# Grouped score matmuls in the mixer, the second token tile on ScalarE's queue, and a later mean product in the two feed-forward stages

## The chip, the core and the metric

The kernel runs on one core of one Trainium2 chip. The metric is the device time of one execution in microseconds (us), the median of several runs. The kernel before took 804.68 us (three runs, 804.41 to 805.51).

## What is computed

One layer of a streaming encoder on 512 tokens of 1024 channels, all in float32:

```
x = x + 0.5 * (silu(h @ w_gate) * (h @ w_up)) @ w_down      # FFN1, h = rms(x) * gain, 1024 -> 2816 -> 1024
x = x + concat(attention(q, k, v), pool(u)) @ w_out         # mixer, [q k v u] = rms(x) * gain @ w_in
x = x + 0.5 * (silu(h @ w_gate) * (h @ w_up)) @ w_down      # FFN2, with its own gain and weights
out = rms(x) * gain
```

The norm is `rms(x) = x * rsqrt(mean(x*x) + 1e-6)` over the channels of a token. The attention has 8 heads of 64 channels. Its queries and keys are normalized head by head, and each chunk of 64 tokens attends to itself and the chunks before it, with a learned bias and a softmax. The pooling branch takes trailing means over 2, 4, 8 and 16 tokens, and a small linear map of them.

## The kernel before

**Products in three parts.** TensorE (PE) multiplies fp32r operands. To reach float32 accuracy each operand is split: ScalarE (ACT) casts it to a high part (line 132, or line 471 in the later half of the feed-forward stages), and VectorE (DVE) subtracts that from the original and gets a low part (line 133 or 476). A product (`mm3`) is then three matmuls, on lines 198 (high, high), 199 and 200 (one low part in each). Channels lie on partitions and tokens in the free dimension, in 8 tiles `x[k]` of 128 channels by 512 tokens; the code calls one such tile a token tile.

**Feed-forward stage (`ffn_up`, used for FFN1 and FFN2).** It begins with four PSUM banks, `first[0..3]`, into which the products of all 8 tiles `k` are added. The weights come in four pieces of 128x1024 (`weights`, for `kp` 0 to 3, two values of `k` each); a piece is asked for on SyncE's queue (line 181), cast by ACT and subtracted by DVE. The very first piece of FFN1 comes in four quarters, so that the first product need not wait for all of it. In FFN1 the tiles of x are asked for between the weight pieces, also on SyncE's queue (line 842). In FFN2 x is already there.

**The norm is applied late.** The products use `x * gain`; the factor of each token, `rb`, is multiplied in afterwards. `acc` collects the squares of x (line 305). `Norm.finish` makes `rb` from it:

```
finish: matmul(wide, mean_of, acc)                   # line 334, PE, the "mean product"
rough:  Ln, Exp, Square                              # lines 318 to 320, ACT
exact:  two scalar_tensor_tensor operations -> rb    # lines 324 and 328, DVE
```

`rb` has two kinds of users, all on DVE: `evacuate`, which empties the `first` banks and those of later plain products (lines 418 and 422; until it has run, the banks are not free for further products), and `norm.blocks`, which scales the eight tiles of x by `rb` (line 359), adds and subtracts blocks of them (line 365) and splits the results into `xa`, `sa` and `ha`, the operands of the rest of the stage. That rest uses, for each group f of 256 columns, seven products on sums of blocks in place of eight; the sums of weight blocks, `wsum`, are made by DVE too (lines 494, 500 and 501). In FFN2 the squares are collected as the mixer's end produces x, so `acc` is nearly ready when the stage begins.

**What sets the order.** Every engine executes its instructions strictly in its program order. In the feed-forward stages a list scheduler of the tile framework puts each engine's instructions in order; what is emitted under `tc.high_priority()` is put ahead of other ready work. In the kernel before, `norm.finish()` is called under it, mean product and all, ahead of the products of `k` = 6. The split tiles, `parts`, have three places; a cast into one waits until PE has used the last weights that lay there.

**Mixer.** Here a planner of the kernel's own (`plan`) lists jobs with costs and ranks, simulates the five engines with the kernel's buffers, among them the 8 PSUM banks (`room`), and writes the order that comes out. `RANK` gives the priorities (the lower first), `SLOW` a factor on the planned costs of ACT and DVE. A score job multiplies the queries of a pair of heads with their keys (line 1528, 64-row operands, results of 64 to 512 columns). It takes 2 banks and consists of 6 matmuls; a pair has 4 of them, 24 matmuls, and there are 4 pairs. The results are evacuated (`evac`), biased, put through a softmax by ACT, transposed by PE (line 1592) and multiplied with v (line 1618). Between the runs of score matmuls PE does products of `mm3` for other heads and for the pooling branch. The planner counts 0.2 us for each change between the two kinds.

Of the kernel before, what the change touches and what calls it, by code (L numbers as in the profile page):

```python
# [8 lines left out]
F32 = mybir.dt.float32  # L9
F32R = mybir.dt.float32r  # L10
I32 = mybir.dt.int32
AF = mybir.ActivationFunctionType
ALU = mybir.AluOpType
# [6 lines left out]
KD = D // P  # L20
# [23 lines left out]
ORDER = (0, "v", 1, "u", "u", "u", "u")  # L44
RANK = dict(
    weights=(-1.0, 0.905, 3.0), qk=2.0, turn=1.1, head=0.9, pool=0.965, map=0.95, u=2.0,
    score=0.5, evac=0.3, bias=1.2, wp=1.1, add=1.1, next=0.965,
)
HOP = 0.45
SLOW = dict(act=1.1, dve=1.06)  # L50
T_MM3 = 0.655
MIX_ENGINES = {
    mybir.EngineType.PE, mybir.EngineType.DVE, mybir.EngineType.Activation, mybir.EngineType.Pool,
# [3 lines left out]
def layer(  # L57
# [31 lines left out]
    nc = tc.nc  # L89
# [39 lines left out]
    def split(src, hi, lo, scale=None):  # L129

        if scale is None:
            nc.scalar.copy(hi, src)  # L132
            nc.vector.tensor_tensor(lo, src, hi.bitcast(F32), op=ALU.subtract)  # L133
        else:
            nc.scalar.activation(hi, src, AF.Copy, scale=scale)
            nc.vector.scalar_tensor_tensor(
                lo, src, scale, hi.bitcast(F32), op0=ALU.mult, op1=ALU.subtract
            )
# [36 lines left out]
    def weights(src, parts=1):  # L175
        n = src.shape[-1]
        raw = raw_tile()
        hi, lo = part_tiles()
        for i in range(parts):
            part = slice(i * n // parts, (i + 1) * n // parts)  # L180
            nc.sync.dma_start(raw[:, part], src[:, part])
            split(raw[:, part], hi[:, part], lo[:, part])
        return hi, lo

    def ordered(acc):
# [16 lines left out]
    def cut(pair, lo, n):  # L202
        return pair[0][:, lo : lo + n], pair[1][:, lo : lo + n]
# [9 lines left out]
    x = residual_tiles()  # L213
    x_d = dram.tile([2 * NT, P, S], F32, name="x_d")

    gain_sb = const.tile([P, 3, KD], F32, name="gain_sb")
    nc.scalar.dma_start(gain_sb, gains)
    ident = const.tile([P, P], F32, name="ident")
    make_identity(nc, ident)
    mean_of = const.tile([P, P], F32R, name="mean_of")  # L220
# [7 lines left out]
    def tables(func, after):  # L228

        if func == AF.Ln:  # L230
            with tc.manual_schedule(engines={mybir.EngineType.Activation}):
                nc.scalar.copy(table, after)
                nc.scalar.preload_act_table_set("natural_log_exp_and_others")
        else:
            nc.scalar.activation(table, after, func, scale=0.0)
# [48 lines left out]
    class Norm:  # L284
# [47 lines left out]
        def finish(self):  # L332
            wide, y, y2 = abank(), temp(), temp()
            nc.tensor.matmul(
                wide.rearrange("p (i a) -> p i a", a=2), mean_of.bitcast(F32),
                self.acc.rearrange("p (a i) -> p i a", a=2), start=True, stop=True,
            )
            self.rough(wide, y, y2)
            tables(AF.Silu, y[:, 0:1])
            self.exact(wide, y, y2)  # L340

        def blocks(self, pool, aside):

# [62 lines left out]
    def ffn_up(norm, wA, down, loaded, in_order, plain, turns=()):  # L406
# [21 lines left out]
        for kp in range(KD // 2):  # L428
            if not loaded:
                load(2 * kp)  # L430
            w = weights(wA[kp], 1 if loaded or kp else 4)
            if not loaded:
                load(2 * kp + 1)
                norm.square(2 * kp)
                norm.square(2 * kp + 1)
            if kp == KD // 2 - 1:
                with tc.high_priority():
                    norm.finish()
            for kk in range(2):
                k = 2 * kp + kk  # L440
                for j in range(4):
                    mm3(first[j], cut(w, (kk * 4 + j) * P, P), norm.h[k], k == 0, k == KD - 1)
        for k in turns:
            z = temp()
            turn_blocks(z, k)
            put_aside(z, k)
# [126 lines left out]
        with tc.manual_schedule(engines={E.PE, E.DVE, E.Activation}):  # L573
            last_silu = last_place = last_sums = nothing
            for n in range(plain, KF):
                f = down.order[n]
                acc, up_lo, up_hi = bank()[:, :HT], bank()[:, :HT], abank()[:, :HT]
                u, z, sg = temp(), temp(), temp()
# [260 lines left out]
    n1, n2, n3 = Norm(0), Norm(1), Norm(2)  # L839

    def load(k):
        nc.sync.dma_start(x[k], xT[k])
        n1.add(k, square=False)


# [15 lines left out]
    with tc.tile_pool(name="act1", bufs=1, reuse_waits="tile") as apool, ExitStack() as in_order:  # L861
# [52 lines left out]
        for g in range(G):  # L914
            now = ahead
# [24 lines left out]
    with tc.tile_pool(name="mix", bufs=1, reuse_waits="tile") as mpool:  # L940
# [12 lines left out]
        class Job:  # L953
            def __init__(self, engine, cost, rank, emit, after, gets, uses, lag, chunk):
                self.engine, self.cost, self.rank, self.emit = engine, cost, rank, emit
                self.after = [z for z in after if z is not None]
                self.gets, self.uses, self.lag, self.chunk = gets, uses, lag, chunk
                self.no, self.then, self.waits, self.ready = len(jobs), [], 0, 0.0

        def job(engine, cost, rank, emit, after=(), gets=(), uses=(), lag=0.0, chunk=None):  # L960
            z = Job(engine, cost, rank, emit, after, gets, uses, lag, chunk)
# [39 lines left out]
        def plan():  # L1001
            free = dict(pe=2.0, act=0.0, dve=0.0, pool=0.0, sp=0.0)
            slots = {what: [-1.0] * n for what, (n, _) in room.items()}
            turn_of = dict(raw=0)
            where, left, open_jobs = {}, dict(held_by), {e: [] for e in free}
            order, times, now = [], [], 0.0
            chunk, scoring, pooling = 0, False, 0.0
            for z in jobs:
                if not z.waits:
                    open_jobs[z.engine].append(z)  # L1010

            def rooms_for(z):
                need, got = {}, []
                for what, key in z.gets:
                    if key in where:
                        continue
                    ready = [t is not None and t <= now for t in slots[what]]
                    n = need.get(what, 0)
                    need[what] = n + 1
                    if what in turn_of:  # L1020
                        i = (turn_of[what] + n) % len(ready)
                        if not ready[i]:
                            return None
                    else:
                        fit = sorted((slots[what][i], i) for i, ok in enumerate(ready) if ok)
                        if len(fit) <= n:
                            return None
                        i = fit[n][1]
                    got.append((what, key, i))
                return got  # L1030

            while len(order) < len(jobs):
                moved = False
                for e in free:
                    if free[e] > now:
                        continue
                    best = None
                    for z in open_jobs[e]:
                        if z.ready > now:
                            continue  # L1040
                        rank = z.rank(chunk) if callable(z.rank) else z.rank
                        if best is None or (rank, z.no) < best[:2]:
                            got = rooms_for(z)
                            if got is not None:
                                best = rank, z.no, z, got
                    if best is None:
                        continue
                    z, got = best[2:]
                    open_jobs[e].remove(z)
                    for what, key, i in got:  # L1050
                        slots[what][i], where[key] = None, (what, i)
                        if what in turn_of:
                            turn_of[what] = (i + 1) % len(slots[what])
                    cost = z.cost * SLOW.get(e, 1.0)
                    if e == "pe":
                        score = z.rank == RANK["score"]
                        cost, scoring = cost + 0.2 * (score != scoring), score
                        chunk = max(chunk, z.chunk or 0)
                    elif e == "pool":
                        pooling = now + cost  # L1060
                    free[e] = now + cost
                    end = now + cost + z.lag + HOP
                    times += [free[e], end]
                    order.append((z, got))
                    z.t0, z.t1 = now, now + cost
                    moved = True
                    for key in z.uses:
                        left[key] -= 1
                        if not left[key]:
                            what, i = where.pop(key)  # L1070
                            slots[what][i] = end
                    for k in z.then:
                        k.waits, k.ready = k.waits - 1, max(k.ready, end if k.engine != e else free[e])
                        if not k.waits:
                            open_jobs[k.engine].append(k)
                if not moved:
                    times = [t for t in times if t > now]
                    now = min(times)
            return order
# [986 lines left out]
```

## Time and profile before

| | |
|---|---|
| median of the runs | 804.68 us (804.41 to 805.51) |
| the profiled execution, its own time | 804.5 us |
| its span in the trace | 802.7 us |
| TensorE busy | 793.5 us (99%) |
| VectorE busy | 709.3 us (88%) |
| ScalarE busy | 499.7 us (62%) |
| GpSimd busy | 152.5 us (19%) |

The span is what the trace covers; 1.8 us of the execution's own time lie outside it. The stages follow each other on PE: the four first banks of FFN1 from 4.8 us, the mixer from about 319 to 483 us, FFN2 from 483 to 796 us, then the last norm and the output. In a row of the timeline stand the start, the duration, the engine, the line, the operation, out<-in by the names of the program, tile and form, the count of like instructions in the row, and in brackets how long the engine was idle before and what ended that. PE is pipelined: a 128x512 matmul lasts 0.38 us in its row but the next begins 0.216 us later (256 columns: 0.11 us).

### The profile page before, as it was taken

The page shows a single profiled execution, that of the slowest core. Times are in us where ns is not written, and L with a number is a line of the kernel's source. Part 1 is how long each engine was busy: PE and PEld are TensorE (multiplying, and loading weights), DVE is VectorE, ACT ScalarE, POOL GpSimd, SP SyncE. Part 2 cuts the span into 40 slices and gives each one's busy share as a digit, 9 for nine tenths or more (in the row PEclk, how much of TensorE's full clock was granted, in tenths as well). Part 3 has the DMA queues.
Part 4 walks back from the last instruction along what each step waited for, and adds up shares of the span by engine and source line. Part 5 has one row for each costly group of instructions (what it writes and reads, how often), then busy time and mean ns, then how long its engine had stood idle before and what let it go on. Part 6 is the DMA issues. An engine that isn't in the chain of part 4 may idle for free.

```text
span 802.7 us, 14916 instructions
## 1 busy us (share of the span) xinstructions
PE 793.5 (99%) x5706; PEld 745.4 (93%) x5706; DVE 709.3 (88%) x1112; ACT 499.7 (62%) x857; POOL 152.5 (19%) x240
## 2 busy tenths in 40 slices
PE   9999999999999999999999999999999999999996
PEld 7889999999999999888888888899999999988986
DVE  7999999999987997778789688999999999986997
ACT  8456655556675675559769545455666655766584
POOL 0023212223220000231444263101110011200010
PEclk9999999999999999999999999999999999999999
DMA  8266889879999675585764867236666457869642
GB/s 291 77 210 210 239 229 245 216 187 259 241 293 317 220 212 156 183 255 100 189 197 81 185 155 204 105 115 205 168 160 195 159 171 175 259 238 343 210 141 105
DMA packets 73848, 158.57 MB, mean 198 GB/s; under 512 B 6560, under 2 KB 31664, under 8 KB 73392
## 3 DMA queue, kind: packets, MB, share of 16 engines
q1 hardware_dynamic: 49808, 109.09, 40.2%
q0 software_dynamic: 23680, 48.24, 28.5%
q8 instruction: 45, 0.74, 0.4%
q10 hardware_dynamic: 288, 0.27, 0.1%
q14 instruction: 27, 0.22, 0.1%
HBM read 153.38 MB, written 50.34 MB: 254 GB/s over the span
## 4 chain that ended last, share of the span: by engine, by line
PE 89%; DVE 5%; issue 1%; DMA 1%; ACT 1%; SPq 0%; DVEq 0%; ACTq 0%
PE mm L200 18%; PE mm L198 18%; PE mm L199 18%; PE a L198 11%; PE a L199 11%; PE a L200 10%; DVE aside L359 1%; PE mm L1528 1%; DVE parts L133 1%; PE mm L1592 1%; DMA raw<-in_wA_dram 1%; DVE aside L365 1%; PE a L1618 1%; PE mm L1618 1%; PE a L1592 0%
## 5 line engine op out<-in xcount | busy, mean ns | idle before, releaser
L565 ACT ACTIVATE t<-mm 128x256 f32<-128x256 f32 x105 | 40.5, 386 | 112.0 <-PE mm L200 110.0
L132 ACT CAST parts<-raw 128x1024 fp32r<-128x1024 f32 (+2 forms) x77 | 74.1, 968 | 51.4 <-PE mm L199 16.6
L133 DVE TENSOR_TENSOR parts<-raw,parts 128x1024 fp32r<-128x1024 f32 (+2 forms) x77 | 85.7, 1121 | 14.8 <-ACT parts L132 14.1
L714 POOL COPY mark<-t 128x1 f32<-128x1 f32 x40 | 16.4, 410 | 331.4 <-DVE t L609 247.7
L199 PE MATMUL mm<-ha,parts 128*128 128x256 f32 x280 | 77.0, 275 | 0.0
L200 PE MATMUL mm<-ha,parts 128*128 128x256 f32 x280 | 77.0, 275 | 0.0
L198 PE MATMUL mm<-ha,parts 128*128 128x256 f32 x280 | 77.0, 275 | 0.0
L716 POOL DMA_DIRECT2D wsum<-in_wB_dram x72 | 70.7, 1114 | 22.5 <-DMA wsum<-wsum 15.0
L476 DVE TENSOR_TENSOR parts<-wsum,parts 128x1024 fp32r<-128x1024 f32 x53 | 64.5, 1218 | 5.1 <-ACT parts L471 5.1
L471 ACT CAST parts<-wsum 128x1024 fp32r<-128x1024 f32 x53 | 53.8, 1046 | 0.8 <-DVE wsum L494 0.4
L198 PEld LDWEIGHTS mm<-ha,parts 128*128 128x128 f32 x280 | 53.8, 192 | 0.1
L199 PEld LDWEIGHTS mm<-ha,parts 128*128 128x128 f32 x280 | 53.8, 192 | 0.1
L200 PEld LDWEIGHTS mm<-ha,parts 128*128 128x128 f32 x280 | 53.8, 192 | 0.0
L133 DVE TENSOR_TENSOR ah<-acts,ah 128x512 fp32r<-128x512 f32 (+1 forms) x72 | 47.1, 662 | 3.0 <-ACT ah L132 2.9
L200 PE MATMUL mm<-hhi,parts 128*128 128x512 f32 x120 | 45.9, 385 | 0.5 <-DVE parts L133 0.5
L198 PE MATMUL mm<-hhi,parts 128*128 128x512 f32 x120 | 45.4, 382 | 0.7 <-DVE t L418 0.3
L199 PE MATMUL mm<-hlo,parts 128*128 128x512 f32 x120 | 46.0, 385 | 0.0
L132 ACT CAST ah<-acts 128x512 fp32r<-128x512 f32 (+1 forms) x72 | 40.8, 580 | 8.3 <-PE mm L199 6.4
L476 DVE TENSOR_TENSOR parts<-raw,parts 128x512 fp32r<-128x512 f32 (+1 forms) x52 | 43.4, 858 | 0.0
L494 DVE TENSOR_TENSOR wsum<-raw 128x1024 f32<-128x1024 f32 x35 | 42.6, 1218 | 0.0
L1116 ACT CAST parts<-raw 128x1024 fp32r<-128x1024 f32 x24 | 25.1, 1046 | 25.8 <-DMA raw<-in_wQK_dram 6.0
L471 ACT CAST parts<-raw 128x512 fp32r<-128x512 f32 (+1 forms) x52 | 39.2, 754 | 2.9 <-DMA raw<-in_wA_dram 2.9
(332 smaller groups left out, 3066.5 us busy)
## 6 DMA issues: line engine op xcount, KB each, us to landing
raw<-in_wA_dram SPq DMA_DIRECT2D x87, 512.0 KB, 4.5
wsum<-in_wB_dram POOLq DMA_DIRECT2D x60, 512.0 KB, 6.9
raw<-wsum SPq DMA_DIRECT2D x36, 512.0 KB, 5.1
raw<-in_wB_dram SPq DMA_DIRECT2D x30, 512.0 KB, 4.7
wsum<-wsum POOLq DMA_DIRECT2D x20, 512.0 KB, 4.5
x<-in_xT_dram SPq DMA_DIRECT2D x16, 256.0 KB, 6.2
raw<-in_wQK_dram SPq DMA_DIRECT2D x8, 512.0 KB, 4.0
wsum<-in_wB_dram POOLq DMA_DIRECT2D x12, 256.0 KB, 6.9
```

Of the source, the lines that this page charges most:

```text
L132: nc.scalar.copy(hi, src)
L133: nc.vector.tensor_tensor(lo, src, hi.bitcast(F32), op=ALU.subtract)
L198: nc.tensor.matmul(acc, a[0], high, start=start, stop=False, **more)
L199: nc.tensor.matmul(acc, a[0], low, start=False, stop=False, **more)
L200: nc.tensor.matmul(acc, a[1], high, start=False, stop=stop, **more)
L471: nc.scalar.copy(hi, src)
L476: nc.vector.tensor_tensor(lo, src, hi.bitcast(F32), op=ALU.subtract)
L494: nc.vector.tensor_tensor(z, raw[:, : 2 * S], raw[:, S : 3 * S], op=ALU.add)
L565: nc.scalar.activation(natural(dst), ordered(src), AF.Copy, scale=scale)
L714: nc.gpsimd.tensor_copy(mark[:, 0:1], after[:, 0:1])
L716: nc.gpsimd.dma_start(self.rows(i, g), self.rows(self.terms[i][at], g), **(dict(accum_op=ALU.add) if at else {}),)
L1116: return lambda: nc.scalar.copy(buf["part", i][0], buf["raw", i])
```

## The change

Four edits:

1. **Mixer.** The rank of `evac` goes from 0.3 to 0.9, and the planned slowness of ACT from 1.1 to 1.06. A new test, `worth`, holds a score job back unless the job before it on PE was a score job too, or enough PSUM banks are free for `GROUP` = 2 score jobs of its pair (or as many as are left of it).
2. **Start of FFN1.** `x[1]` is asked for on ScalarE's queue, behind the gains, and no longer on SyncE's.
3. **First quarter of the first weight piece.** Its cast goes from ACT to DVE (`tensor_copy`). Everything else in `weights` stays.
4. **Mean product.** `norm.finish()` is called after the first product (three matmuls) of `k` = 6 rather than ahead of all of them, and only what follows the mean product (`rough`, the Silu table, `exact`) stands under `tc.high_priority()`. This holds for FFN1 and FFN2.

```
-    score=0.5, evac=0.3, bias=1.2, wp=1.1, add=1.1, next=0.965,
+    score=0.5, evac=0.9, bias=1.2, wp=1.1, add=1.1, next=0.965,
-SLOW = dict(act=1.1, dve=1.06)
+GROUP = 2
+SLOW = dict(act=1.06, dve=1.06)
...
-            split(raw[:, part], hi[:, part], lo[:, part])
+            if i == 0 and parts > 1:
+                nc.vector.tensor_copy(hi[:, part], raw[:, part])
+                nc.vector.tensor_tensor(
+                    lo[:, part], raw[:, part], hi[:, part].bitcast(F32), op=ALU.subtract
+                )
+            else:
+                split(raw[:, part], hi[:, part], lo[:, part])
...
     nc.scalar.dma_start(gain_sb, gains)
+    nc.scalar.dma_start(x[1], xT[1])
...
-            self.rough(wide, y, y2)
-            tables(AF.Silu, y[:, 0:1])
-            self.exact(wide, y, y2)
+            with tc.high_priority():
+                self.rough(wide, y, y2)
+                tables(AF.Silu, y[:, 0:1])
+                self.exact(wide, y, y2)
...
-            if kp == KD // 2 - 1:
-                with tc.high_priority():
-                    norm.finish()
             for kk in range(2):
                 k = 2 * kp + kk
                 for j in range(4):
                     mm3(first[j], cut(w, (kk * 4 + j) * P, P), norm.h[k], k == 0, k == KD - 1)
+                    if (kp, kk, j) == (KD // 2 - 1, 0, 0):
+                        norm.finish()
...
-        nc.sync.dma_start(x[k], xT[k])
+        if k != 1:
+            nc.sync.dma_start(x[k], xT[k])
...
+            def worth(z):
+                if scoring or z.engine != "pe" or z.rank != RANK["score"]:
+                    return True
+                more = min(GROUP, sum(k.t0 is None for k in of_pair[z.uses[0]]))
+                return sum(t is not None and t <= now for t in slots["bank"]) >= 2 * more
...
-                        if best is None or (rank, z.no) < best[:2]:
+                        if (best is None or (rank, z.no) < best[:2]) and worth(z):
```

In the changed kernel the same code has other line numbers: `mm3` 205 to 207, the mean product 342, `rough` 326 to 328, `exact` 332 and 336, scores 1549, splits 134 and 137.

**PE at the start of FFN2.** In the listings the tile numbers are unique: mm_6109 to mm_6112 are the four first banks, hhi_5900, hhi_5915 and so on to hhi_6025, hhi_6079 and hhi_6094 are the tiles of x in the order of use, acc_5908 is the sum of squares, a_6203 (6206) the mean product's bank. Before, the mean product stands 16 matmuls into the stage:

```order
L200 MATMUL mm_6112<-hhi_5900,parts 128x512
L198 MATMUL mm_6109<-hhi_5915,parts 128x512
L199 MATMUL mm_6109<-hlo_5916,parts 128x512
L200 MATMUL mm_6109<-hhi_5915,parts 128x512
L198 MATMUL mm_6110<-hhi_5915,parts 128x512
L334 MATMUL a_6203<-acc_5908,mean_of 128x512
L199 MATMUL mm_6110<-hlo_5916,parts 128x512
L200 MATMUL mm_6110<-hhi_5915,parts 128x512
```

Now it stands behind the first product of `k` = 6:

```order
L207 MATMUL mm_6112<-hhi_6025,parts 128x512
L205 MATMUL mm_6109<-hhi_6079,whi_6198 128x512
L206 MATMUL mm_6109<-hlo_6080,whi_6198 128x512
L207 MATMUL mm_6109<-hhi_6079,wlo_6199 128x512
L342 MATMUL a_6206<-acc_5908,mean_of 128x512
L205 MATMUL mm_6110<-hhi_6079,whi_6198 128x512
L206 MATMUL mm_6110<-hlo_6080,whi_6198 128x512
```

It was PE's row 3465 and is now its row 3524: 59 matmuls later, not three, since before it was put ahead of products that the program names first.

**DVE at the same place.** raw_6141 and raw_6197 are weight pieces of the first banks, raw_6269, raw_6302 and raw_6363 those of the next plain products, raw_6375 the one whose block sums wsum_6415 and wsum_6439 are. Before:

```order
L133 TENSOR_TENSOR parts<-raw_6141,parts 128x1024
L133 TENSOR_TENSOR wlo_6199<-raw_6197,whi_6198 128x1024
L928 STREAM_TRANSPOSE t_6238<-x_2849 128x512
L928 STREAM_TRANSPOSE t_6244<-x_2849 128x512
L324 SCALAR_TENSOR_TENSOR t_6205<-a_6203,t_6205 128x512
L133 TENSOR_TENSOR parts<-raw_6269,parts 128x1024
L328 SCALAR_TENSOR_TENSOR rb_6212<-t_6205,t_6204 128x512
L359 SCALAR_TENSOR_TENSOR aside_6264<-x_2846,gain_sb,rb_6212 128x512 x2
L359 SCALAR_TENSOR_TENSOR aside_6264<-x_2847,gain_sb,rb_6212 128x512 x2
L133 TENSOR_TENSOR parts<-raw_6302,parts 128x1024
```

Now:

```order
L134 TENSOR_TENSOR parts<-raw_6141,parts 128x1024
L134 TENSOR_TENSOR wlo_6199<-raw_6197,whi_6198 128x1024
L134 TENSOR_TENSOR parts<-raw_6269,parts 128x1024
L134 TENSOR_TENSOR parts<-raw_6302,parts 128x1024
L134 TENSOR_TENSOR parts<-raw_6363,parts 128x1024
L502 TENSOR_TENSOR wsum_6415<-raw_6375 128x1024
L937 STREAM_TRANSPOSE t_6238<-x_2849 128x512
L332 SCALAR_TENSOR_TENSOR t_6208<-a_6206,t_6208 128x512
L937 STREAM_TRANSPOSE t_6244<-x_2849 128x512
L336 SCALAR_TENSOR_TENSOR rb_6215<-t_6208,t_6207 128x512
L508 TENSOR_TENSOR wsum_6439<-wsum_6415,raw_6375 128x512
L427 TENSOR_TENSOR t_6250<-mm_6109,rb_6215 128x512
```

Three weight splits and two sums of weight blocks that stood behind the first operation of `exact` now stand at it or ahead of it; every scaling of x stands behind it as before.

In the mixer, PE's score matmuls stood in 8 runs of 6, 18, 6, 12, 6, 24, 18 and 6; in the changed kernel they stand in 5 runs of 18, 6, 24, 24 and 24.

More of the change, by code (lines that the diff above doesn't have):

```diff
@@ L958, in __init__ @@
                 self.no, self.then, self.waits, self.ready = len(jobs), [], 0, 0.0
+                self.t0 = self.t1 = None
         def job(engine, cost, rank, emit, after=(), gets=(), uses=(), lag=0.0, chunk=None):
@@ L1007, in plan @@
             chunk, scoring, pooling = 0, False, 0.0
+            of_pair = {}
+            for z in jobs:
+                if z.engine == "pe" and z.rank == RANK["score"]:
+                    of_pair.setdefault(z.uses[0], []).append(z)
+            def worth(z):
[3 more added lines that the diff above has]
+                return sum(t is not None and t <= now for t in slots["bank"]) >= 2 * more
             for z in jobs:
```

## The prediction

> **What bounds the kernel now.** I read the busy shares of the page first, then its chain of work that ended last.
>
> ```profile
> span 802.7 us, 14916 instructions
> PE 793.5 (99%) x5706; PEld 745.4 (93%) x5706; DVE 709.3 (88%) x1112; ACT 499.7 (62%) x857; POOL 152.5 (19%) x240
> PE 89%; DVE 5%; issue 1%; DMA 1%; ACT 1%; SPq 0%; DVEq 0%; ACTq 0%
> ```
>
> PE is busy all the time, so only two things move the end: fewer microseconds of PE work, or PE waiting for somebody. Only 9 us are not PE. The candidate for making PE wait is DVE at 88%, and an average hides where it is full. So I took the windows table by stage; the columns are window, length, then busy time of PE, PE's weight loads, DVE, ACT and POOL, then the granted clock, DMA share and GB/s.
>
> ```profile
> 420.00:440.00 20.00, 20.00 (x124) 17.59 (x121) 18.62 (x57) 18.30 (x45) 9.11 (x12) 1.00 0.45 80
> 480.00:500.00 20.00, 19.95 (x90) 16.60 (x89) 16.20 (x21) 10.90 (x14) 9.45 (x15) 1.00 0.69 188
> 500.00:520.00 20.00, 19.67 (x91) 16.93 (x90) 19.96 (x26) 8.83 (x12) 2.64 (x2) 1.00 0.28 95
> 520.00:540.00 20.00, 20.00 (x151) 19.07 (x150) 19.71 (x30) 13.35 (x23) 1.70 (x4) 1.00 0.44 142
> ```
>
> From 500 to 540 us, the start of FFN2, DVE idles 0.33 us in 40: there is no room, and any time that DVE loses just before is not made up there. In the mixer ACT and DVE are both above 90%. These two places and FFN1's start are what the change touches.
>
> **FFN2, the mean product.** The timelines of PE, ACT and DVE there:
>
> ```profile
> 486.76 1.34 PE L334 MATMUL a<-acc,mean_of 128*128 128x512 f32 x2
> 505.70 0.45 PE L198 MATMUL mm<-hhi,parts 128*128 128x512 f32 x1 [0.33 <-DVE t L418]
> 538.95 0.28 PE L200 MATMUL mm<-xa,parts 128*128 128x256 f32 x1
> ...
> 488.20 0.69 ACT L318 ACTIVATE t<-a,eps 128x512 f32<-128x512 f32 x1
> 489.99 0.72 ACT L319 ACTIVATE t<-t,less_ln 128x512 f32<-128x512 f32 x1
> 491.55 0.62 ACT L320 ACTIVATE t<-t 128x512 f32<-128x512 f32 x1
> 494.83 1.05 ACT L132 CAST parts<-raw 128x1024 fp32r<-128x1024 f32 x1 [1.14 <-PE mm L199]
> 500.01 1.05 ACT L132 CAST parts<-raw 128x1024 fp32r<-128x1024 f32 x1 [4.13 <-PE mm L199]
> ...
> 492.48 0.65 DVE L324 SCALAR_TENSOR_TENSOR t<-a,t 128x512 f32<-128x512 f32 x1
> 514.97 1.22 DVE L133 TENSOR_TENSOR wlo<-raw,whi 128x1024 fp32r<-128x1024 f32 x1
> 537.11 1.22 DVE L476 TENSOR_TENSOR parts<-wsum,parts 128x1024 fp32r<-128x1024 f32 x1
> ...
> L494 DVE TENSOR_TENSOR wsum<-raw 128x1024 f32<-128x1024 f32 x35 | 42.6, 1218 | 0.0
> ```
>
> The order moves the mean product back by 59 matmuls. At 0.216 us each that is 12.7 us; PE is otherwise back to back, so it runs at about 499.5 in place of 486.76. Nothing in between depends on it. The Ln began 1.44 us after the mean product started (488.20 - 486.76); then come 0.69 + 0.72 + 0.62 us of ACT, now in one piece, because the casts stand ahead of them. So the first operation of `exact` can start at 499.5 + 1.44 + 2.03, about 503.0, in place of 492.48: 10.5 us later. If casts still fell between, it would be the old distance, 492.48 - 486.76 = 5.72, hence 505.2.
>
> DVE works in order, and what does it do meanwhile? The new order puts three splits and one sum of weights ahead of `exact`, but the second and third split wait for casts, and those casts wait for PE to free a place of `parts` (the two rows with 1.14 and 4.13 of idle time). PE no longer has the 1.34 us of the mean product ahead of them, so the casts run about 1.3 us earlier than before, at 493.5 and 498.7, and end 1 us later. DVE is through with the first split at about 492.4 (it takes the place of the transposes that ended at 492.48). It idles to 494.5 (2.1 us), works 1.2, idles to 499.7 (4.0 us), works 1.2 on the split, 1.2 on the sum and 0.65 on a transpose, and waits 0.3 for the ACT chain. Together 6.4 us of idle time that was not there before; the 0.33 us of old idle time in the full stretch behind it absorb a little. **DVE runs about 6.0 us late** from here on. The other way of counting agrees: from 492.48 to the end of the `wlo` split, 516.2, DVE had 23.7 us of work; three splits (3 x 1.14 from start to start) leave this stretch, and a transpose and a half sum (0.65 each, as 128x512 forms take) come in, 21.6 in all. So `wlo` is ready at 503.0 + 21.6 = 524.6, 8.4 late, of which a sum and a half sum done in advance (1.2 + 0.65) are no loss: 6.5.
>
> Where does PE feel it? First the next bank is freed late. DVE needs five 128x512 operations from 503.0 to the end of the evacuation, 3.2 us, so PE's row of 505.70 comes at about 506.3: 0.6 us. Then PE, to which the order gives 21 matmuls of another bank first, comes 75 rows (16.1 us) later to the matmul that needs `wlo`, at 522.4; undisturbed it would be 521.8. `wlo` comes at 524.6. That is 0.6 + 2.2 = **2.8 us, the floor**. Next comes the split of a sum, 537.11 + 1.22 = 538.33, which PE uses at 538.95: it had 0.62 to spare. DVE is 6.0 late there, because its stretch has no gap, so PE loses 6.0 - 0.6 = **5.4 us in all**, 2.8 of them already paid. From there on DVE may catch up, but PE, back to back, gives nothing back. Without any spare it would be 6.0; with `exact` at 505.2, 7.6.
>
> I take +5.4, with 2.8 and 7.6 as ends.
>
> **Mixer.** Score matmuls use 64 rows and bank pairs, and each switch between them and the others costs PE time. From PE's timeline, one pair whose scores stand in three runs, and one with a single run of 24:
>
> ```profile
> 365.40 0.38 PE L200 MATMUL a<-parts,hlo 128*128 128x512 f32 x1
> 366.92 0.38 PE L199 MATMUL a<-parts,hhi 128*128 128x512 f32 x1
> 367.13 0.38 PE L200 MATMUL a<-parts,hlo 128*128 128x512 f32 x1
> 368.77 0.38 PE L199 MATMUL a<-parts,hhi 128*128 128x512 f32 x1
> 368.99 0.38 PE L200 MATMUL a<-parts,hlo 128*128 128x512 f32 x1
> 370.17 0.38 PE L199 MATMUL a<-parts,hhi 128*128 128x512 f32 x1
> ...
> 415.00 0.38 PE L200 MATMUL a<-hhi,parts 128*128 128x512 f32 x1
> 417.76 0.38 PE L199 MATMUL a<-hlo,parts 128*128 128x512 f32 x1
> ...
> 422.04 0.44 PE L1592 MATMUL mm<-ident,prob 128*128 128x128 f32 x2
> ```
>
> In each pair of rows (the last row apart) the first is the matmul ahead of a run, the second the second matmul behind it; their distance less two ordinary steps (0.43) is what the run takes. Three runs: 1.09 + 1.21 + 0.75 = 3.05. One run: 2.76 - 0.43 = 2.33. Two splits cost 0.72, one 0.36. Of 8 runs, 5 remain: 3 x 0.36 = **1.1 us saved**, if nobody waits for it. The bounds: 0 if banks or softmax push back exactly as much, 1.1 at the best; beyond that see the third rival.
>
> **FFN1.** PE, DVE, ACT and SyncE's queue at the start and at the end of the first banks:
>
> ```profile
> 10.86 0.48 PE L198 MATMUL mm<-hhi,parts 128*128 128x512 f32 x1
> 21.07 0.38 PE L199 MATMUL mm<-hlo,parts 128*128 128x512 f32 x1
> 21.84 1.34 PE L334 MATMUL a<-acc,mean_of 128*128 128x512 f32 x2 [0.39 <-DVE acc L305]
> 50.00 0.38 PE L199 MATMUL mm<-hlo,parts 128*128 128x512 f32 x1
> 50.88 0.48 PE L200 MATMUL mm<-hhi,parts 128*128 128x512 f32 x1 [0.49 <-DVE parts L133]
> ...
> 25.36 0.69 DVE L324 SCALAR_TENSOR_TENSOR t<-a,t 128x512 f32<-128x512 f32 x1 [0.64 <-ACT t L320]
> ...
> 9.76 1.05 ACT L132 CAST parts<-raw 128x1024 fp32r<-128x1024 f32 x1 [0.18 <-DMA raw<-in_wA_dram]
> ...
> 3.08 0.91 SPq L842 DMA_DIRECT2D x<-in_xT_dram  x2
> ```
>
> Two x tiles take 0.91 us of issue on SyncE's queue, so without `x[1]` everything behind it is asked for 0.46 us earlier; the second weight piece, for which ACT waited 0.18 and on which PE's product at 10.86 hangs, comes earlier by 0 to 0.46. The cast of the first quarter, now on DVE, may start the first product some 0.3 us earlier, but that ends in the same wait at 10.86 and is worth nothing by itself.
>
> Before, PE stood still 0.56 us for `acc` (21.84 - 21.07 - 0.216). The mean product now comes four matmuls later, at 22.15 less the 0.46, when `acc` is there. That saves PE the wait, but it does not last: DVE's chain from the mean product's result to the split at 50.88 has no gap behind 25.36, and PE waits there (0.66). What is gained by the end of that wait is what the order lets PE do ahead of it, two more matmuls (0.43), less the chain's shift, +0.31 - 0.46 = -0.15. So 0.6 if the second piece is early by all of 0.46, 0.1 if by nothing; I take **0.5 saved**.
>
> Against the x tile on its own queue speaks the Trainium skill, page "DMA: Bandwidth & Descriptors", section "Queues, rings and completion order": a DMA engine takes turns between queues packet by packet, so `x[1]` would share the engines with `x[0]` and the first quarter, which then land later. By that rule the first product would be later rather than earlier and FFN1 would gain about 0.1, not 0.5; the trace of before has only the gains on that queue and cannot show it.
>
> **Sum.** The profiled execution took 804.5, its span 802.7 and 1.8 around it, 0.2 under the median 804.68, which is nothing. 804.5 + 5.4 - 1.1 - 0.5 = **808.3 us**. A measurement of this kernel tells about 0.2%, 1.6 us, from no change: faster is below 803.1, slower above 806.3.
>
> **Rivals.**
>
> *A: PE pays only the floor.* If DVE finds its lost time again between 524 and 538, for instance because parts it does there wait less, PE loses 2.8: 804.5 + 2.8 - 1.1 - 0.5 = 805.7, no difference. For it speaks that DVE's order there is rewritten too; against it, 19.71 of 20 us busy, work that doesn't shrink. Chance 0.12.
>
> *B: the late mean product is covered altogether (the other side).* DVE would have to deliver `wlo` by 521.8, hence `exact` at 500.2, 2.8 us sooner than I work out. That needs casts that find free places of `parts` early enough for DVE to have no idle time. Then 804.5 - 1.1 - 0.5 = 802.9: faster. Against it stand the two waits of 1.14 and 4.13 us in ACT's rows, which come from PE's own order. Chance 0.08.
>
> *C: the scores become too dense.* With 24 score matmuls at once ACT's softmax gets eight banks in a lump, at 18.30 of 20 us busy. If the transposes behind it wait, PE loses one score job of evacuation and softmax, some 1 to 2 us, instead of saving 1.1: 804.5 + 5.4 - 0.5 + 0.5 = 809.9. It decides as soon as PE reaches a pair's transposes less than about 4.3 us behind its scores (422.04 - 417.76, the first transpose behind the run of 24). For it: that near-full ACT; against it: the order leaves such a distance after the new runs too. Chance 0.12.
>
> *D: the clock drops.* PE's clock falls after an idle stretch, as the end of the kernel shows:
>
> ```profile
> 795.97 0.28 PE L200 MATMUL a<-parts,ah 128*128 128x256 f32 x1
> ...
> 798.00:800.00 2.00, 0.00 (x0) 0.00 (x0) 0.67 (x3) 0.72 (x1) 0.00 (x0) 0.94 0.47 176
> 800.00:803.00 3.00, 0.00 (x0) 0.00 (x0) 0.00 (x0) 0.00 (x0) 0.00 (x0) 0.50 0.34 128
> ```
>
> PE's last matmul ends at 796.25. A mean of 0.94 in a 2 us window with half speed at its end means half speed from about 799.8, 3.5 us after it. My waits in FFN2 are 2.2 and 2.6 us, each shorter; if they fall into one of over 3.5, PE works at half speed for about as long again and loses half of it, 1.7: 810.0. Chance 0.06.
>
> The Trainium skill, page "TensorE: Matmul & The Clock Gate", section "Part 1: The HAM clock gate (the "warmup" mystery)", has the gate as a free-running window of about 3.4 us, after whose idle passing the clock is halved; the 3.5 us of the trace agree.
>
> That the edit doesn't do what it says is certain in FFN2: three products by the program's text are 59 matmuls in the order. The forecast itself has 0.62.
>
> **Range and chances.** The forecast's own spread is 805.7 (floor) to 810.5 (with 7.6). A lies inside the low end and C and D at the high end; leaving B and the tails out gives 805.2 to 811.0. Faster: B and a little, 0.09. Same: A and the forecast's lowest, 0.14. Slower: 0.77.
>
> **What would show it.** In the changed kernel's trace: the mean product of FFN2 near 499 on its PE timeline; two idle gaps of about 2 and 4 us on DVE between 491 and 500, ended by ACT's casts; `wlo` ready near 524.6 and PE waiting there about 2 us, then again about 2.6 us near 541 for a split of a sum; PE's idle total up by about 5. In the mixer 5 score runs and no wait at the transposes. In FFN1 no wait ahead of the mean product and PE's position after 51 about 0.5 ahead. The forecast is wrong if DVE has no gaps at 492 to 500, or if PE passes 524 and 541 without waiting.

## The result: 810.82 us, and the profile after

The changed kernel takes 810.82 us (median of 6 runs, 809.51 to 812.67) against 804.63 (6 runs, 804.41 to 805.51). The ratio is 1.0077, with a 95% interval of 1.0064 to 1.0091: slower, by some 6.2 us. The profiled execution took 810.97 us with a span of 809.2. The page's head and chain:

```profile
span 809.2 us, 14915 instructions
PE 794.6 (98%) x5706; PEld 747.0 (92%) x5706; DVE 708.6 (88%) x1113; ACT 499.3 (62%) x856; POOL 148.3 (18%) x240
PE 88%; DVE 7%; DMA 2%; ACT 1%; issue 1%; POOL 0%; DVEq 0%; ACTq 0%
```

PE has the same 5706 matmuls and nearly the same busy time; 6.5 us of span are time in which it waits or runs slowly. The windows by stage of the changed kernel (same columns as in the prediction):

```profile
480.00:500.00 20.00, 19.44 (x90) 16.55 (x89) 9.94 (x11) 8.16 (x10) 4.23 (x7) 1.00 0.63 195
500.00:520.00 20.00, 19.13 (x86) 15.90 (x85) 19.44 (x29) 10.05 (x14) 6.63 (x10) 1.00 0.22 44
520.00:540.00 20.00, 17.70 (x110) 15.94 (x109) 20.00 (x26) 10.57 (x18) 0.96 (x2) 0.91 0.34 109
540.00:560.00 20.00, 19.51 (x174) 19.29 (x173) 19.46 (x30) 12.29 (x22) 2.07 (x6) 1.00 0.60 208
```

DVE works 9.9 us from 480 to 500, where it worked 16.2 before, and then is all but full, 19.44 and 20.00 of 20, while PE idles. And PE's clock, 1.00 in these windows before, is 0.91 in one of them. The timelines of PE, ACT and DVE at this place:

```profile
489.44 0.48 PE L207 MATMUL mm<-hhi,parts 128*128 128x512 f32 x1 [0.56 <-DVE parts L134]
500.12 1.24 PE L342 MATMUL a<-acc,mean_of 128*128 128x512 f32 x2
506.77 0.45 PE L205 MATMUL mm<-hhi,parts 128*128 128x512 f32 x1 [0.87 <-ACT whi L133]
525.39 0.48 PE L207 MATMUL mm<-hhi,wlo 128*128 128x512 f32 x1 [2.30 <-DVE wlo L134]
543.41 0.38 PE L207 MATMUL a<-xa,parts 128*128 128x256 f32 x1 [0.49 <-DVE parts L484]
...
494.28 1.05 ACT L133 CAST parts<-raw 128x1024 fp32r<-128x1024 f32 x1 [3.38 <-PE mm L206]
499.46 1.04 ACT L133 CAST parts<-raw 128x1024 fp32r<-128x1024 f32 x1 [4.13 <-PE mm L206]
501.40 0.69 ACT L326 ACTIVATE t<-a,eps 128x512 f32<-128x512 f32 x1 [0.90 <-PE a L342]
...
495.36 1.23 DVE L134 TENSOR_TENSOR parts<-raw,parts 128x1024 fp32r<-128x1024 f32 x1 [3.01 <-ACT parts L133]
500.54 1.23 DVE L134 TENSOR_TENSOR parts<-raw,parts 128x1024 fp32r<-128x1024 f32 x1 [3.95 <-ACT parts L133]
503.54 0.69 DVE L332 SCALAR_TENSOR_TENSOR t<-a,t 128x512 f32<-128x512 f32 x1
524.12 1.21 DVE L134 TENSOR_TENSOR wlo<-raw,whi 128x1024 fp32r<-128x1024 f32 x1
542.14 1.22 DVE L484 TENSOR_TENSOR parts<-wsum,parts 128x1024 fp32r<-128x1024 f32 x1
```

Read from the middle: two casts of ACT wait for PE to give a place of `parts` free, DVE stands still 3.01 and 3.95 us for their results, and the operations on `rb` are queued behind. DVE has not got that time back at 542. Before, the split of the last row stood here:

```profile
535.64 1.22 DVE L476 TENSOR_TENSOR parts<-wsum,parts 128x1024 fp32r<-128x1024 f32 x1
```

So DVE is 6.5 us late there. PE waits for DVE at 525.39 and, for the last time that is long in this stretch, at 543.41. The wait at 506.77 is put down to an ACT cast, which ends at the same moment but which this matmul doesn't read; what it needs is the bank that DVE empties at 505.94 to 506.62.

To see where the time went I compared when PE starts the same amount of matmul work in the two traces (nominal durations summed over its rows). The changed kernel is later by 0.6 us at the end of FFN1, wins 0.74 in the mixer (it enters FFN2 0.12 early), loses 6.12 in FFN2 up to 543 us, and 0.45 more at a single wait near 747 us; about 6.5 in all, the difference of the two spans. That last piece varies from run to run, 0 to 0.6 us in the kernels below, and is not put down to the change.

### The profile page after: what moved, and what is told of

It is laid out like the page before. It is cut to its first block, busy times and chain, and to the rows that moved or that the text cites. A ratio compares the mean times of both kernels' runs of the same rounds, so it can differ in the third digit from the quotient of the medians.

```text
span 809.2 us, 14915 instructions
## 1 busy us (share of the span) xinstructions
PE 794.6 (98%) x5706; PEld 747.0 (92%) x5706; DVE 708.6 (88%) x1113; ACT 499.3 (62%) x856; POOL 148.3 (18%) x240
## 4 chain that ended last, share of the span: by engine, by line
PE 88%; DVE 7%; DMA 2%; ACT 1%; issue 1%; POOL 0%; DVEq 0%; ACTq 0%
PE mm L207 18%; PE mm L205 18%; PE mm L206 18%; PE a L207 10%; PE a L206 10%; PE a L205 10%; DMA raw<-in_wA_dram 1%; DVE aside L368 1%; DVE aside L374 1%; PE mm L1549 1%; PE mm L1639 1%; DVE parts L134 1%; PE a L1613 1%; DVE acts L733 1%; DVE xa L137 1%
## 5 line engine op out<-in xcount | busy, mean ns | idle before, releaser
L722 POOL COPY mark<-t 128x1 f32<-128x1 f32 x40 | 14.3, 357 | 328.7 <-DVE t L617 247.9
L1142 DVE TENSOR_TENSOR parts<-raw,parts 128x1024 fp32r<-128x1024 f32 x24 | 29.5, 1231 | 14.4 <-ACT parts L1137 14.4
```

The lines of the kernel that those rows point to most:

```text
L722: nc.gpsimd.tensor_copy(mark[:, 0:1], after[:, 0:1])
L1142: nc.vector.tensor_tensor(lo, buf["raw", i], hi.bitcast(F32), op=ALU.subtract)
```

## Experiments

**Undo the late mean product in FFN2, keep everything else.** In FFN2 `finish` is called under high priority ahead of `k` = 6 again:

```
+            if kp == KD // 2 - 1 and not (not loaded):
+                with tc.high_priority():
+                    norm.finish()
...
-                    if (kp, kk, j) == (KD // 2 - 1, 0, 0):
+                    if (not loaded) and (kp, kk, j) == (KD // 2 - 1, 0, 0):
                         norm.finish()
```

Expected: 

> The changed kernel with one thing undone: in FFN2 the mean product is again put ahead of the products of k = 6 under high priority (in FFN1 it stays late). Theory (the late mean product of FFN2 starves VectorE and costs 6.1 us): the time falls from 810.8 by about 6.1 to 804.7, range 804.0 to 805.3, and VectorE's gaps of 3.0 and 3.95 us before 500.5 are gone. Rival (the loss comes from the denser scores or from the start of FFN1, and FFN2 only shows it): the time stays above 808.

Measured: 804.87 us against 805.23 (11 and 33 runs), ratio 0.9999 (0.9990 to 1.0008). The loss is gone. In the window and on DVE's timeline of this kernel the gaps are gone too:

```profile
480.00:500.00 20.00, 19.95 (x90) 16.59 (x89) 16.41 (x22) 10.90 (x15) 9.43 (x15) 1.00 0.70 188
...
492.27 0.65 DVE L332 SCALAR_TENSOR_TENSOR t<-a,t 128x512 f32<-128x512 f32 x1
```

DVE works 16.41 us there, not 9.94, and `exact` starts at 492.27, not 503.54. The rest of the change together is worth nothing that can be measured. So the late mean product in FFN2 is the cause of the loss, whatever the way from it to PE.

**The mixer's edit alone** (the two ranks and factors, `GROUP` and `worth`, on the kernel before).

Expected: 

> The kernel before with the mixer's edit alone. Theory (fewer switches between scores and other matmuls, 0.74 us by the two traces, 1.1 by the sum of the prediction): 804.6 - 0.7 = 803.9, range 803.4 to 804.3. Rival (eight banks at once make ScalarE's softmax late): 805 or more, with waits of TensorE at the transposes.

Measured: ratio 0.9991 (0.9982 to 1.0000), 804.45 against 805.23, that is 0.7 us less, at the edge of what can be told from no change. The traces agree more sharply than the times: from 300 us to the mixer's end the PE lag falls by 0.79 here, 0.74 in the changed kernel, 0.77 in the kernel above, and by 0.0 to 0.04 in kernels that keep the old mixer.

**The two edits at the start alone** (`x[1]` on ScalarE's queue, first quarter's cast on DVE).

Expected: 

> The kernel before with x[1] on ScalarE's queue and the first quarter's cast on VectorE, nothing else. Theory of the prediction (requests behind x[1] go out 0.46 us earlier, worth 0 to 0.5): 804.1 to 804.6. Rival, from the trace of the changed kernel (its first product starts at 5.23 and not 4.81, since the first quarter lands later beside x[1]; the second piece is hardly earlier): 804.6 + 0.4 to 0.6, about 805.1.

Measured: ratio 1.0012 (1.0003 to 1.0020), 806.32 against 805.23: 1.0 us slower. PE's mean product and ACT at the norm of FFN1 in this kernel:

```profile
21.23 1.35 PE L341 MATMUL a<-acc,mean_of 128*128 128x512 f32 x2 [0.40 <-DVE acc L312]
...
23.34 0.72 ACT L326 ACTIVATE t<-t,less_ln 128x512 f32<-128x512 f32 x1
23.97 1.03 ACT L132 CAST parts<-raw 128x1024 fp32r<-128x1024 f32 x1
24.90 0.63 ACT L327 ACTIVATE t<-t 128x512 f32<-128x512 f32 x1
...
26.17 0.68 DVE L331 SCALAR_TENSOR_TENSOR t<-a,t 128x512 f32<-128x512 f32 x1
```

The mean product is 0.6 us earlier than before (21.84), as the prediction wanted. But the edits changed the order elsewhere: a weight cast now stands between the Exp and the Square, the split that needs it stands ahead of `exact` on DVE, and `exact` starts at 26.17 and not at 25.36. The gain of 0.6 became a loss of 0.8 on the chain that PE waits for at 51 us.

**The late mean product in FFN1 alone.**

Expected: 

> The kernel before with the late mean product in FFN1 alone. Theory of the prediction: TensorE's wait of 0.56 for acc goes, but the wait at 50.88 for VectorE's split takes most of it back: 804.6 - 0.1 to - 0.5, about 804.3. Rival (VectorE's chain from the later mean product is the longer way, 0.3 later): 804.9.

Measured: ratio 1.0006 (0.9997 to 1.0014): no difference that can be told. PE's timeline:

```profile
21.70 0.38 PE L200 MATMUL mm<-hhi,wlo 128*128 128x512 f32 x1
21.92 1.24 PE L334 MATMUL a<-acc,mean_of 128*128 128x512 f32 x2
...
50.92 0.70 PE L200 MATMUL mm<-hhi,parts 128*128 128x512 f32 x2 [0.76 <-DVE parts L133]
```

The 0.56 us of waiting ahead of the mean product is gone and is paid at 50.92, where PE resumes at the same time as before (50.88) with two matmuls more behind it. What was left at 52 us, 0.15 us, went at a wait near 63 us. The interval leaves open whether there is a small loss.

**Each edit of the start by itself.** Expected of the queue move: 

> The kernel before with x[1] asked for on ScalarE's queue and nothing else. Theory (the second weight piece comes 0.5 us earlier, but the order puts a weight cast between Ln and Exp of the mean, so rb is late by 0.4 to 0.9 and the split at 51 us with it): +0.4 to +0.9 us. Rival (the queue move is a gain and the other edit of the start, the cast on VectorE, brings the loss): -0.5 us.

Expected of the cast: 

> The kernel before with the first quarter's cast on VectorE and nothing else. Its order leaves Ln, Exp and Square in one piece. Theory (the loss at the start comes from the queue move): within 0.2 us of the kernel before. Rival (the cast on VectorE brings it): +0.6 to +1.0 us.

Measured: 1.0003 (0.9994 to 1.0012) and 1.0002 (0.9993 to 1.0011). Neither can be told from no change, and which of them makes the 1.0 us of both together stays open. In the order of the queue move alone a cast does stand between Ln and Exp, and `exact` starts late there; with the cast on DVE alone it doesn't stand there:

```profile
24.27 1.04 ACT L132 CAST parts<-raw 128x1024 fp32r<-128x1024 f32 x1
26.62 0.69 DVE L325 SCALAR_TENSOR_TENSOR t<-a,t 128x512 f32<-128x512 f32 x1
```

So the traces point to the queue move, and the times don't confirm it.

**A smaller delay of the mean product.** The kernel before, with FFN2's mean product behind the first product of `k` = 4:

```
+            with tc.high_priority():                 # in finish(), around rough, tables, exact
...
-            if kp == KD // 2 - 1:
+            if kp == KD // 2 - 1 and not (loaded):
...
+                    if (loaded) and (kp, kk, j) == (2, 0, 0):
+                        norm.finish()
```

Expected: 

> The kernel before with one thing changed: in FFN2 the mean product stands behind the first product of k = 4, so 35 matmuls later than before (59 in the changed kernel). Theory (VectorE idles while it waits for casts that wait for TensorE; TensorE pays VectorE's lateness less 0.6): mean product near 494.3, first operation of exact near 497.8, VectorE idles 2.1 us for one cast and 0.8 for the chain, 2.9 in all; TensorE loses 2.9 - 0.6 = 2.3 at most, so 0.2 to 0.3% above the kernel before, about +2.0 us. Rival (the loss goes with the delay of the mean product itself, 6.1 us for 59 matmuls): 35/59 of 6.1, +3.6 us. Rival (the clock's fall is what costs): no pause of TensorE over 2 us, no fall, +0.5 us or less.

Measured: ratio 1.0047 (1.0034 to 1.0059), 808.27 against 805.11, which is some 3.8 us: the +3.6 of the first rival fits the interval, the theory's +2.0 doesn't. DVE's gaps:

```profile
495.57 1.23 DVE L133 TENSOR_TENSOR parts<-raw,parts 128x1024 fp32r<-128x1024 f32 x1 [2.99 <-ACT parts L132]
498.58 0.69 DVE L324 SCALAR_TENSOR_TENSOR t<-a,t 128x512 f32<-128x512 f32 x1 [0.56 <-ACT t L320]
```

They sum to 3.55 us (2.9 expected), and less 0.62 that gives 2.9. In the trace PE loses 2.6 between 484 and 560 us, near what DVE's gaps give. Its last matmul comes 3.6 later; the rest was lost ahead of 26 us, where this edit leaves the order as it was, and at the wait near 744 that varies from run to run. So the trace speaks for DVE's gaps, but the times alone would speak for the rival, and five runs don't settle it. The second rival is out: the clock stays at 1.00 and the loss is there.

**More work on DVE, the mean product where it was.** The kernel before, with ten dummy additions behind `rb` in FFN2:

```
+            if self.which == 2:
+                for _ in range(10):
+                    z = temp()
+                    nc.vector.tensor_tensor(z, self.rb, y, op=ALU.add)
```

Expected: 

> The kernel before, its mean product where it was, with ten additions of 128x512 on VectorE behind rb in FFN2, whose results nobody uses: 10 x 0.6 = 6.0 us of lateness of VectorE and nothing else. Theory (lateness of VectorE at this place is enough): TensorE loses 6.0 - 0.6 = 5.4 us, +0.67%, about the loss of the changed kernel's FFN2. Rival (VectorE's lateness is made good before TensorE needs it; the loss in the changed kernel comes from TensorE's own order): +3 us or less.

Measured: ratio 1.0088 (1.0075 to 1.0102), 812.26 against 805.11. In the trace PE loses 6.7 us in FFN2, not 5.4. The direction is right, a later DVE is enough; the size is not. Nor is this lateness and nothing else: the list scheduler also moved 13 of PE's matmuls from 524 to 517 us and set the evacuations on DVE among the scalings of x. PE, DVE and one window of this kernel:

```profile
522.07 0.48 PE L200 MATMUL mm<-hhi,parts 128*128 128x512 f32 x1 [3.17 <-DVE parts L133]
...
532.91 0.69 DVE L422 TENSOR_TENSOR t<-mm,rb 128x512 f32<-128x512 f32 x1 [0.80 <-PE mm L200]
...
524.00:526.00 2.00, 2.00 (x7) 1.53 (x6) 2.00 (x4) 0.62 (x1) 0.00 (x0) 0.50 0.83 234
```

After the pause of 3.17 us PE runs at half clock from 523 to 526 us, and behind that DVE waits for PE (0.80 at 532.91), not the other way. Here the fall of the clock should cost.

**Fill the pause.** To tell what the clock's fall costs, unused 256-column matmuls were put ahead of the products that follow the plain ones, into a bank that is overwritten next; 22 in the changed kernel, 40 in the kernel with the dummy additions:

```
+                if loaded and n == plain:
+                    spare = norm.h[KD - 1][0]
+                    for _ in range(22):
+                        nc.tensor.matmul(
+                            up_hi, spare[:, :P], spare[:, :HT], start=True, stop=True,
+                            skip_group_check=True,
+                        )
                 product(acc, w11, A11, True)
```

Expected of the changed kernel so filled: 

> The changed kernel with 22 extra 256-column matmuls on TensorE (their results are overwritten unread), most of them just ahead of the matmul that waits for wlo near 525 us, so that the pause of 2.5 us there is mostly filled. Theory (the clock's fall behind that pause is covered, since TensorE waits for VectorE at 543 anyway): the clock stays at 1.00 and the time stays at the changed kernel's, 0.7 to 0.8% above the kernel before; TensorE's wait near 543 grows from 0.66 to about 2.3 us. Rival (the fall of the clock costs its 1.7 us): the time is 1.7 us, 0.2%, shorter, 0.5 to 0.6% above.

Measured: ratio 1.0073 (1.0060 to 1.0087), against 1.0077 unfilled: the same. PE's two waits and a window, filled:

```profile
525.10 0.48 PE L207 MATMUL mm<-hhi,wlo 128*128 128x512 f32 x1 [0.40 <-DVE wlo L134]
543.12 0.38 PE L207 MATMUL a<-xa,parts 128*128 128x256 f32 x1 [0.70 <-DVE parts L484]
...
527.00:528.00 1.00, 1.00 (x6) 0.88 (x5) 1.00 (x2) 0.94 (x2) 0.00 (x0) 1.00 0.99 387
```

and the same window of the changed kernel, with its neighbour:

```profile
526.00:527.00 1.00, 1.00 (x5) 0.79 (x4) 1.00 (x3) 0.62 (x1) 0.00 (x0) 0.61 0.57 66
527.00:528.00 1.00, 1.00 (x4) 0.81 (x3) 1.00 (x3) 0.42 (x1) 0.00 (x0) 0.50 0.81 311
```

The clock stays at 1.00, and still PE is held by DVE until 543.12. The wait there grew to 0.87 us between neighbours and not to the 2.3 expected: another wait, of 1.1 us near 532.5, for an operation of ACT, took the rest. From 484 to 560 us PE loses 6.09 us, against 6.12 with the fall. So the fall costs nothing here that can be told, because DVE's lateness sets the end.

Expected of the other: 

> The kernel with ten more additions on VectorE, with 40 extra 256-column matmuls that fill most of TensorE's pause near 518 to 522 us. In the unfilled kernel the clock fell to a half from 523 to 526 us and VectorE waited for TensorE behind it, so there the fall was not covered. Theory: the clock stays at 1.00 and the loss shrinks from 6.7 us (in the trace, from 484 us on) to the 5.4 that VectorE's lateness explains. Rival (the loss is VectorE's alone): 6.7 us again.

Measured: ratio 1.0068 (1.0056 to 1.0081), against 1.0088 unfilled: about 1.6 us less, though the intervals meet. The clock, in the window that showed 0.50:

```profile
524.00:526.00 2.00, 2.00 (x11) 1.62 (x10) 2.00 (x3) 0.33 (x1) 0.00 (x0) 1.00 0.23 20
```

In the trace PE loses 5.7 us in FFN2, of which 0.67 are six of the fill matmuls that came too late to fall into the pause; without them 5.1, against the 5.4 expected. The whole execution that was profiled was not shorter, 811.90 against 811.82 us; it lost 1.5 us at a single wait near 207 us, in FFN1, where the two kernels are the same. So the fall seems to be paid where PE and not DVE is the later one behind the pause: this stretch of the trace shows it, the times don't settle it.

## Why the prediction was right, and where its sizes were off

The forecast was slower, 808.3 us in 805.2 to 811.0; it is 810.8, at the upper end. The cause and its place are the ones that it named. Its sum was 2.5 us short. By the trace, FFN2 cost 0.7 more, the mixer gained 0.4 less, FFN1 came out 1.1 worse, and 0.45 was lost near 747. That the time still lies in the range, by 0.2 us, is partly luck: the upper end was set for rivals C and D, and neither price was paid.

- **FFN2, +5.4 forecast, +6.1 measured.** The order's 59 matmuls, the two gaps of DVE ended by ACT's casts, `exact` (503.54; 503.0 forecast), `wlo` (ready at 525.33; 524.6) and PE's wait for it (2.46 us between neighbours; 2.2) are as forecast. The step that was too small: "nothing in between depends on it", that PE gets through the 59 matmuls back to back. It waits 0.7 us at 489.44 for a weight split; before, the mean product stood ahead of that matmul and covered the wait. So the mean product starts at 500.12, not 499.5, and PE frees the places of `parts` later: the first gap of DVE is 3.01 us, not 2.1. DVE's lateness is 6.5, not 6.0, and the loss goes with it.
- **The second wait, 2.6 us forecast near 541, is 0.66 at 543.** The clock's fall took its place: half speed from 526.2 to 529.6 costs 1.7 us which PE would else have waited. The rival with the clock gave it 0.06 and added its price to the sum; it came true in its mechanism, its price was covered. It was held to need a pause of over 3.5 us; one of 2.46 was enough (the last section shows what the 3.5 was).
- **Mixer, -1.1 forecast, -0.74 measured.** A run of 24 costs what it did before; first row the matmul ahead of it, second the second one behind, 2.76 - 0.43 = 2.33 again:

```profile
415.20 0.38 PE L207 MATMUL mm<-hhi,parts 128*128 128x512 f32 x1
417.96 0.38 PE L206 MATMUL mm<-hlo,parts 128*128 128x512 f32 x1
...
375.20 0.38 PE L207 MATMUL mm<-parts,hlo 128*128 128x512 f32 x1
375.71 0.45 PE L205 MATMUL mm<-parts,hhi 128*128 128x512 f32 x1
```

  The last two rows show what took a part back: 0.29 us of standstill (0.51 less a step of 0.216) behind the run of 24 at 370 us, which is in no trace of the old mixer and in every one of the new, between 374.7 and 375.8. The trace names nothing that ended it, and it stands ahead of a product and not of a transpose, so that it is the softmax of rival C is not shown. Rival C's own sum has a slip: a loss of 1 to 2 us in place of the gain would give 810.4 to 811.4, not 809.9.
- **FFN1, -0.5 forecast; no gain.** In the profiled execution it is +0.6; but kernels whose FFN1 is unchanged show +0.2 to +1.6 in single traces, so the times decide: +1.0 us (0.3 to 1.6) for the edits of the start, nothing for the mean product. The rows of PE and DVE in the changed kernel:

```profile
5.23 0.67 PE L205 MATMUL mm<-hhi,parts 128*128 128x512 f32 x2 [0.74 <-DVE parts L184]
12.02 0.48 PE L207 MATMUL mm<-hhi,parts 128*128 128x512 f32 x1 [0.56 <-DVE parts L134]
...
4.79 0.29 DVE L184 CAST parts<-raw 128x256 fp32r<-128x256 f32 x1 [3.77 <-DMA raw<-in_wA_dram]
26.12 0.69 DVE L332 SCALAR_TENSOR_TENSOR t<-a,t 128x512 f32<-128x512 f32 x1 [1.78 <-ACT t L328]
```

  and the same cast in the kernel that has it on DVE with `x[1]` still on SyncE's queue:

```profile
4.05 0.29 DVE L183 CAST parts<-raw 128x256 fp32r<-128x256 f32 x1 [3.03 <-DMA raw<-in_wA_dram]
```

  Two steps failed. The first quarter lands later: its cast waits for the transfer until 4.79, without the queue move until 4.05, so the first product is later (5.23, before 4.81) and not earlier. That is what the prediction drew from the Trainium skill, page "DMA: Bandwidth & Descriptors", section "Queues, rings and completion order", and these rows agree in the later landing; turns packet by packet no run shows. And the step "the chain's shift, +0.31 - 0.46 = -0.15" was wrong in sign: `exact` starts at 26.12, 0.76 later than before. Here that comes from PE's wait at 12.02 and the later mean product; with the edits of the start alone it came from a cast that slid into the norm's ACT chain.

What stays open: which edit of the start costs its 1.0 us, and why DVE's split of `wlo`, which PE waits for near 747 us, comes late in some traces.

## What to carry to other kernels

An instruction that leaves a high-priority block is not moved past the next three lines of the program but past all that the priority had put it ahead of: look at its place in the instruction order. A cheap operation whose result gates an in-order engine that is full afterwards has to be early; what that engine idles before is paid by whoever waits for it, less the slack there, here 0.6 us. Before a standstill is counted as a gain, look for the next waits on the same chain: in FFN1 they took back all of 0.56 us.

## What the runs showed of the hardware

PE's clock fell to a half after pauses of 2.46 us (changed kernel; PE resumed at 525.39) and 3.4 us (dummy additions; resumed at 522.07). PE was already working again when the fall came, 0.8 and 1.0 us after it resumed. With pauses of 1.32 us (the smaller delay) and of 0.56 us (the filled kernel) it stayed at 1.00. The changed kernel's windows, then PE's first pause and the windows with the additions:

```profile
529.00:530.00 1.00, 1.00 (x5) 0.81 (x4) 1.00 (x3) 0.47 (x1) 0.00 (x0) 0.68 0.68 264
806.00:807.00 1.00, 0.00 (x0) 0.00 (x0) 0.00 (x0) 0.00 (x0) 0.00 (x0) 0.56 0.93 348
...
518.52 0.38 PE L198 MATMUL mm<-ha,parts 128*128 128x256 f32 x1 [0.96 <-ACT ha L132]
523.00:524.00 1.00, 1.00 (x4) 0.79 (x4) 1.00 (x2) 0.00 (x0) 0.00 (x0) 0.54 0.00 0
526.00:527.00 1.00, 1.00 (x5) 0.85 (x4) 1.00 (x2) 0.14 (x1) 0.00 (x0) 0.75 1.01 393
806.00:807.00 1.00, 0.00 (x0) 0.00 (x0) 0.03 (x1) 0.32 (x1) 0.00 (x0) 0.69 0.12 43
```

The granted clock places each change within its window: 0.61 from 526 to 527 means half speed from 526.22, 0.68 from 529 to 530 until 529.63, and 0.56 from 806 to 807 a fall near 806.1, when PE's work is over. With the additions the changes lie at 523.08, 526.49 and 806.38. Each slow stretch lasts 3.41 us, and the last fall comes 276.48 and 279.89 us after it by the trace's own clock records, 81 and 82 times 3.4133. In the records of all twelve traces every change lies a whole number of such steps behind the first record. So the clock changes on a grid of 3.413 us. In the step that ended at the fall PE stood still for 2.46 us (changed kernel) and 2.40 us (additions, from 519.67 to 522.07); in the step ahead of the latter it stood still for 2.16 us, 1.13 ahead of the matmul at 518.52 and 1.03 behind it, and the clock stayed. In these traces it is thus the idle time within one step that decides, somewhere between 2.16 and 2.40 us, and not the length of a pause; three such steps are few. The 3.5 us of the trace of before, from the last matmul to the fall, reach to the end of a step and are no threshold.

The Trainium skill, page "TensorE: Matmul & The Clock Gate", section "Part 1: The HAM clock gate (the "warmup" mystery)", has the clock halved after at least one idle window of about 3.4 us that runs freely, and restored after a busy one as long. The grid and the slow stretches agree with that; the windows that halved the clock here were idle for 2.40 and 2.46 us and not throughout.
